# Splitting the first layer of a two-layer decoder step into two passes over the tokens, so that output projection and MLP of the first half may run beside the recurrent heads of the second

## The chip, the cores and the metric

One Trainium2 chip, all 8 cores, every core running the same program on its own prompt (2048 tokens) and 16 of the 128 sample tokens. The time is device microseconds (us) of the slowest core. A program on all cores has a second, slower state in some executions, in which the cores of a die get a lower clock. Ratios and their intervals below are of fast executions alone, against the kernel before in the same rounds. A median quoted for a run is over all its executions as the record has it; without the slow ones it changes by 1.3 us at most (late2, 1588.77 instead of 1590.04). The experiments ran in several rounds and on several chips, and the kernel before had fast medians of 1613.4 to 1614.8 us there, so a difference of a microsecond or two between two runs is not to be read. PE is TensorE, PEld its weight load, DVE VectorE, ACT ScalarE, POOL GpSimd, SP SyncE.

## The reference, cut to what matters

```python
def even_layer(h, ...):                          # layer 0; ... marks cuts
    proj = h @ w_in                              # 1024 -> 256 pool + 4 x 768
    pool_out, pool_new = pool_mix(u, ...)        # windows 2/4/8/16
    logf = jnp.log(lb32 + (1.0 - lb32) * jax.nn.sigmoid(fz32))
    k = (1.0 - lb32) * jax.nn.sigmoid(-fz32)
    v = jax.nn.silu(iz)
    o, s_new = hgrn2_chunked(q, k, v, logf, s_prev)   # 6 heads, 128 x 128 state, causal
    o = o * lax.rsqrt(jnp.mean(o * o, axis=-1, keepdims=True) + EPS)
    ...
    return jnp.concatenate([pool_out, o], axis=-1) @ w_out, pool_new, s_new

def trunk(x, ...):
    for l in range(2):
        h = rmsnorm(x, norm_mix[l])
        x = x + (even_layer if l == 0 else odd_layer)(h, ...)   # odd: a gated convolution of width 3
        h = rmsnorm(x, norm_mlp[l])
        x = x + jnp.square(jax.nn.relu(h @ ff_w1[l])) @ ff_w2[l]
    return rmsnorm(x, norm_final), ...
```

A tile is 512 tokens, so a prompt has tiles 0 to 3. A head's state runs through the tiles in order. Everything after the heads (projection, norm, MLP) is independent from token to token: that is what the change uses.

## The kernel before

The kernel is a generator of instructions. Each job (a head's work on one tile, a pool unit, the MLP) is a coroutine that yields operations. A list scheduler with a cost model picks, at each step, the operation that can start earliest by its estimates, and by priority where several are within 0.03 us. The result is one fixed order for each engine; on the chip each engine works its order off and waits, by semaphore, wherever an operand isn't there yet. So an estimate decides what stands behind what.

A unit is one head on one tile. It works in a context (five 2 KB pages a partition) and, at first, a gate buffer (three pages). Part of these pages lie in the arena, part in the place of x blocks ("x_sb"), which are reloaded later:

```python
def units():                                     # before
    for group in HEAD_GROUPS:                    # (0, 1), (2, 3), (4, 5)
        for t in range(4):
            for h in group:
                yield loaded(U_HEAD + h)
                yield h0(t)                      # tile t is normalised and transposed
                c = yield from take_c()          # one of 4 contexts
                itg = yield Alloc(gpool)
                # ... spawn core, gthread, vthread, gate at priorities 10 n .. 10 n + 3
                n += 1
```

The end of a unit, with the state, its write-out and the output:

```python
            yield STT(Sst[:, h, :], js(c.N, 2), c.r[:, 3:4], js(bank(kS), 3), ALU.mult, ALU.add, ...)
            flags.add(("S", h, t))
            # ... output matmuls
            if t == 3:
                yield ACT(js(c.N, 0), Sst[:, h, :], AF.Copy, [B_S[h]] + c.Br, c.BN, scale=c.r[:, 4:5])
                yield DMA("sp", misc(), [(nhp[h], js(c.N, 0))], c.BN, (), 65536)   # reads page N of the context
            yield ACT(c.kd, bank(ko), AF.Square, [B_ps[ko]], c.Bkd)
            # ...
            yield ACT(c.N, bank(km), AF.Ln, [B_ps[km]], c.BN, bias=EPS)            # writes page N again
            # ...
            yield STT(mixT[:, 2 + h, tokslice(t)], bank(ko), hcols[:, GAIN + h:GAIN + h + 1], c.lg, ALU.mult, ALU.mult, ...)
```

And the sequence of the dense parts, at the lowest priority (300):

```python
        def main():
            yield up(("G", HEAD_GROUPS[-1][-1], 2))
            banks.reserve([2, 3])
            yield from outproj(U_WO, 1, "mix")   # all 17 blocks: tiles 0 to 3 and the samples
            # ...
            mlp(U_FF0, 1, 2)                     # 8 steps x 5 tiles
            # ... conv, second projection, second MLP
```

Of the kernel before, what the change touches and what calls it, by code (L numbers as in the profile page):

```python
# [8 lines left out]
BF16 = mybir.dt.bfloat16  # L9
# [7 lines left out]
EPS = 1e-6  # L17
NSLOT = 5
NPG = 14
NXPG = 24  # L20
JUNK = [12, 13]
# [10 lines left out]
HEAD_GROUPS = [(0, 1), (2, 3), (4, 5)]  # L32
BLOCKS = list(range(17))
LAST_ORDER = (4, 0, 1, 2, 3)
LOAD_ORDER = [0, 1, 2, 3, 4, 5, 6] + list(range(7, 51))
LOAD_GATE = {1: 3, 2: 11, 3: 15, 4: 15}
XGATE = {b: (0,) for b in range(4, 16)}
POOLPRIO = -5
SMPPRIO = -5

U_HEAD = 0
U_POOL = 6
U_WO = 7
U_FF0 = 9
U_CONV = 25
U_OO = 33
U_FF1 = 35
NU = 51
# [308 lines left out]
def build():  # L357
# [40 lines left out]
    with ExitStack() as es:  # L398
# [174 lines left out]
        slot_pool = Pool([(i, [B_ring[i]]) for i in range(NSLOT)])  # L573

        def loader():
            for u in LOAD_ORDER:
                it = yield Alloc(slot_pool)
                s = it[0]
                ncol = unit_cols[u]
                pairs = [(ring[:, s, c0:min(c0 + 2048, ncol)], wst[u, :, c0:min(c0 + 2048, ncol)])  # L580
                         for c0 in range(0, ncol, 2048)]
                gate = LOAD_GATE.get(u)
                if gate is not None:
                    yield up(("x", gate))
                yield DMA("pool", ring_ds[s], pairs, [B_x[gate]] if gate is not None else [], [B_ring[s]], ncol * 512)
                slot_of[u] = s

        def loaded(*us):
            return Until(lambda: all(u in slot_of for u in us))

        def drop(u):
            s = slot_of.pop(u)
            slot_pool.give((s, [B_ring[s]]))

        def used(u, n):
            uses[u] = uses.get(u, 0) + 1
            if uses[u] == n:
                drop(u)
# [8 lines left out]
        def setup():  # L607
            yield from xload(0)
            yield DMA("sp", misc(), [(identb[:, :], c_identb), (gcols[:, :], gcols_d)], (), [B_const], 50000)
            flags.add("const")  # L610
            yield from xload(1)
            yield DMA("sp", misc(), [(lbl[:, :], lbl_d), (hcols[:, 18:24], gain_d)], (), [B_lbl, B_hcols], 12000)
            flags.add("small")
            yield from xload(2)
            yield from xload(3)
# [26 lines left out]
        def setup3():  # L642
            yield DMA("pool", ones_ds, [(onesb[:, :], c_onesm)], (), [B_ones], 65536)
            flags.add("ones")
            yield Until(lambda: U_HEAD + 2 in slot_of)
# [7 lines left out]
        junks = Pool([((i, JUNK[i]), [B_pg[JUNK[i]][0], B_pg[JUNK[i]][1]]) for i in range(len(JUNK))])  # L653
# [79 lines left out]
        def make_g(p0):  # L733
            g = Ctx()
            g.a, g.b, g.c = (pgf(p0 + k) for k in range(3))
            g.Ba, g.Bb, g.Bc = (list(B_pg[p0 + k]) for k in range(3))
            g.bufs = flat(pgb(p0, 3))
            return g
# [44 lines left out]
        def gthread(h, t, sl, c, g, key):  # L783
# [31 lines left out]
            gpool.give((g, g.bufs))  # L815
# [88 lines left out]
        NCU = 24 + 8 + 2  # L904

        def cgive(c):

            cpool.give((c, c.bufs))
            if cwait[0] == 0:
                for q in list(cpool.avail):  # L910
                    cpool.avail.remove(q)
                    for p in range(q[0].p0, q[0].p0 + 5):
                        flags.add(("pgdone", p))
                    cdone[0] += 1

        cwait = [NCU]
        cdone = [0]

        def take_c():
            it = yield Alloc(cpool)  # L920
            cwait[0] -= 1
            if cwait[0] == 0:
                for q in list(cpool.avail):
                    cpool.avail.remove(q)
                    for p in range(q[0].p0, q[0].p0 + 5):
                        flags.add(("pgdone", p))
                    cdone[0] += 1
            return it[0]

        def units():  # L930
            n = 0
            for group in HEAD_GROUPS:
                for t in range(4):
                    for h in group:
                        yield loaded(U_HEAD + h)
                        yield h0(t)
                        if n == 0:
                            yield up("hcols", "ones")
                        c = yield from take_c()
                        itg = yield Alloc(gpool)  # L940
                        sl = slot_of[U_HEAD + h]
                        key = (h, t)

                        def wrap(gen, h=h):
                            yield from gen
                            used(U_HEAD + h, 13)
                        S.spawn(core(h, t, c, key), 10 * n)
                        S.spawn(wrap(gthread(h, t, sl, c, itg[0], key)), 10 * n + 1)
                        S.spawn(wrap(vthread(h, t, sl, c, key)), 10 * n + 2)
                        S.spawn(wrap(gate(h, t, sl, c, key)), 10 * n + 3)  # L950
                        n += 1

        def gdone():
            yield Until(lambda: len(gpool.avail) == len(Gs) and ("G", HEAD_GROUPS[-1][-1], 3) in flags)
            for p0 in GPAGES:
                for p in range(p0, p0 + 3):
                    flags.add(("pgdone", p))
# [4 lines left out]
        def sample_hgrn():  # L962
            for gi, group in enumerate(HEAD_GROUPS):
                for h in group:
                    yield from sample_head(h)
# [3 lines left out]
        def sample_head(h):  # L969
            yield loaded(U_HEAD + h)  # L970
# [3 lines left out]
            sl = slot_of[U_HEAD + h]  # L974
# [4 lines left out]
            for g in range(4):  # L979
                yield DMA("sp", misc(), [(Sh[:, 4 * g:4 * g + 4, :], st_hgrn[4 * g:4 * g + 4, h].rearrange("b k v -> k b v"))],  # L980
                          (), pgb(shp + g), 262144)
# [12 lines left out]
            used(U_HEAD + h, 13)  # L994
# [27 lines left out]
            for g in range(4):  # L1022
# [9 lines left out]
                Bg = pgb(shp + g)  # L1032
                Sg = Sh[:, 4 * g:4 * g + 4, :]
# [8 lines left out]
                yield ACT(sbg, Sh[:, 4 * g:4 * g + 4, :], AF.Copy, Bg, Bsb)  # L1042
                yield MMG([(bank(ko)[:, 4 * g + i:4 * g + i + 1], sbg[:, i, :], qT[:, 4 * g + i:4 * g + i + 1], True, True)
# [14 lines left out]

        def pool_mixer(cch):
            yield loaded(U_POOL)  # L1060
            yield up("wblk")
            yield up(*[("h0", b) for b in range(17)])
            sl = slot_of[U_POOL]
            for t in range(4):
                yield from pool_unit(cch, t, sl)
            yield from pool_sample(cch, sl)

        def pool_unit(c, t, sl):
            cx = yield from take_c()
# [68 lines left out]
            cgive(cx)  # L1138
# [10 lines left out]
        def pool_sample(c, sl):  # L1149
            cx = yield from take_c()  # L1150
# [10 lines left out]
            used(U_POOL, 2)  # L1161
# [31 lines left out]
            cgive(cx)  # L1193


        def outproj(u0, norm_n, tag):
            yield loaded(u0, u0 + 1)
            s0, s1 = slot_of[u0], slot_of[u0 + 1]
            for b in BLOCKS:
                t = b // 4  # L1200
                yield up(*[(tag, c, t) for c in range(8)])
                if norm_n == 1 and b < 16 and b >= 16 - NXPG // 2:
                    yield up(("xback", b))
                it = yield Alloc(PB)
                p = it[0]
                pp = psT[p]
                tk = slice(b * 128, (b + 1) * 128) if b < 16 else slice(NT, NTOK)
                np_ = 128 if b < 16 else 16
                mms = []
                for half, s in ((0, s0), (1, s1)):  # L1210
                    for kc in range(8):
                        mms.append((pp[0:np_, half * 512:(half + 1) * 512], mixT[:, kc, tk],
                                    ring[:, s, kc * 512:(kc + 1) * 512], kc == 0, kc == 7))
                yield MMG(mms, mixb(t) + [B_ring[s0], B_ring[s1]], it[1])
                flags.add((tag + "used", b))

                def fin(b=b, p=p, it=it, np_=np_, pp=pp):
                    xb = x_sb[:, b, :] if b < 16 else xs_sb[0:16, :]
# [3 lines left out]
                S.spawn(fin(), 250)  # L1222
            drop(u0)
            drop(u0 + 1)


        hid = [[pgf(HIDP + 2 * i + n // 2).bitcast(BF16)[:, (n % 2) * 512:(n % 2 + 1) * 512] for n in range(4)]
               for i in range(NHID)]
        B_hid = [[B_pg[HIDP + 2 * i + n // 2][n % 2] for n in range(4)] for i in range(NHID)]
# [3 lines left out]
        def mlp(u0, n_in, n_out):  # L1233
            mtag = "m%d" % n_in
            steps = [(s, t) for s in range(8) for t in ((0, 1, 2, 3, 4) if s < 7 else LAST_ORDER)]
            hin = "h%d" % n_in
            pk_of = {}
            pi = 0
            for (s, t) in steps:
                if t < 4:  # L1240
                    pk_of[(s, t)] = pi
                    pi += 1

            def ff1():
                for s, t in steps:
                    yield loaded(u0 + 2 * s)
                    sl = slot_of[u0 + 2 * s]
                    yield up(*([(hin, b) for b in range(4 * t, 4 * t + 4)] if t < 4 else [(hin, 16)]))
                    if t < 4:
                        q = pk_of[(s, t)]  # L1250
                        if q >= NHID:
                            yield up((mtag, "hfree", q - NHID))
                        hb, Bh = hid[q % NHID], B_hid[q % NHID]
# [34 lines left out]
                    used(u0 + 2 * s, 5)  # L1288

            def ff2():  # L1290
                for s, t in steps:
                    yield loaded(u0 + 2 * s + 1)
                    sl = slot_of[u0 + 2 * s + 1]
                    if t < 4:
                        q = pk_of[(s, t)]
                        yield up(*[(mtag, "hid", q, n) for n in range(4)])
                        hb, Bh = hid[q % NHID], B_hid[q % NHID]
# [303 lines left out]
```

## Time and profile before

| | before |
|---|---|
| median of 4 runs | 1613.45 us (1612.48 to 1614.44) |
| profiled spans of the 8 cores | 1601.0 to 1610.6 us |
| granted clock, mean of a core | 0.980 to 0.984 |
| end of the first MLP, over the cores | 872.8 to 878.4 us, median 876.0 |

The prediction shows the main lines of the profile and reads them; three more are needed here. They are from the page of the kernel before: the queue of the weight loads (packets, MB, share of 16 DMA engines), the bytes read, and the loads of the weight ring (count, size, median us to landing).

```profile
q0 software_dynamic: 15008, 50.93, 18.9%
...
HBM read 124.20 MB, written 15.54 MB: 87 GB/s over the span
...
ring<-wst POOLq DMA_DIRECT2D x93, 512.0 KB, 8.4
```

The weight stream has room on average: its packets took less than a fifth of the time of the 16 DMA engines.

Two countings recur below. *PE work* is the number of matmuls times 217 ns for 512 columns, 61 ns for 128 and 30 ns for the small ones, close to the prediction's yardstick (an estimate: 32 of 512 columns take 6.94 us, 32 of 128 are listed with 1.95). *Lost* is a stretch's length less that work. It counts idle PE and low clock alike. The yardstick is a little generous: the 1.95 us include the modelled end of the last matmul, and from start to start the medians in these traces are 216, 56 and 25 ns. By the medians, more is lost in each stretch; the second set of numbers below says how much. The trace of before lacks 159 of 8932 matmul records, so its work up to the end of the first MLP is taken from the changed kernel's complete trace: 786.6 us, the same matmuls (the counts by size agree, but for 88 missing ones of 512 columns).

### The profile page before, as it was taken

The numbers are of one execution on the slowest core, as the hardware profiler recorded it, in microseconds if no ns is written. First come the engines' busy times: TensorE is split into PE (matmuls) and PEld (weight loads), VectorE is DVE, ScalarE is ACT, GpSimd is POOL, SyncE is SP. The second block draws the span as 40 slices with busy tenths as digits, with TensorE's granted clock in tenths as the row PEclk, the third lists the DMA queues.
The fourth block names the chain that finished last, engine by engine and source line by source line (L and its number), as shares of the span: only waits on it lengthen the run. The fifth ranks groups of instructions, "written<-read, shape, count | busy, mean of one in ns | idle before, by whom it ended". The sixth has DMA issues, their size and how long they took to land.

```text
span 1610.6 us, 23082 instructions; the slowest of 8 cores (1601.0 to 1610.6 us)
## 1 busy us (share of the span) xinstructions
PE 1512.9 (94%) x8773; PEld 742.5 (46%) x8932; DVE 935.7 (58%) x1396; ACT 603.6 (37%) x1222; POOL 179.7 (11%) x210
## 2 busy tenths in 40 slices
PE   3897698999999999999999999999999999999997
PEld 2554354555444444444445434445444444444443
DVE  4898686976454444444457555556544454444457
ACT  4786476876311111111148222236311111111135
POOL 1246733410000000000000000000000000000000
PEclk9898799999999999999999999999999999999999
DMA  9624235044321121122022023330320221121013
GB/s 238 138 61 89 62 78 112 29 89 127 52 53 27 27 53 31 22 52 47 1 40 40 4 40 50 55 66 1 53 53 8 45 53 27 27 53 27 1 54 157
DMA packets 51751, 90.32 MB, mean 56 GB/s; under 512 B 5422, under 2 KB 32924, under 8 KB 51644
## 3 DMA queue, kind: packets, MB, share of 16 engines
q0 software_dynamic: 15008, 50.93, 18.9%
q1 hardware_dynamic: 36636, 37.91, 7.7%
q8 instruction: 74, 1.21, 0.3%
q14 instruction: 33, 0.27, 0.1%
HBM read 124.20 MB, written 15.54 MB: 87 GB/s over the span
## 4 chain that ended last, share of the span: by engine, by line
PE 85%; DVE 6%; DMA 4%; ACT 2%; issue 2%; POOL 1%; SPq 0%; ACTq 0%; DVEq 0%; POOLq 0%
PE pp L516 83%; PE pp L526 2%; DVE arena L497 1%; DVE x_sb L485 1%; DVE arena L485 1%; DMA x_sb<-xp 1%; DMA ring<-wst 1%; ACT arena L472 1%; DMA nhp<-x_sb 1%; ACT x_sb L472 1%; DMA ncp<-arena 1%; DVE x_sb L497 0%; DMA ncs<-arena 0%; POOL x_sb L485 0%; SPq L531 0%
## 5 line engine op out<-in xcount | busy, mean ns | idle before, releaser
L516 PE MATMUL pp<-hT,ring 128*128 128x512 bf16 (+1 forms) x4018 | 792.0, 349 | 9.9 <-ACT arena L472 2.0
L516 PEld LDWEIGHTS pp<-hT,ring 128*128 128x128 bf16 x4112 | 353.2, 98 | 408.6 <-issue 29.8
L472 ACT ACTIVATE arena<-pp 128x512 bf16<-128x512 f32 (+4 forms) x370 | 211.5, 575 | 760.6 <-PE pp L516 732.8
L485 DVE TENSOR_TENSOR x_sb<-x_sb,pp 128x1024 f32<-128x1024 f32 (+1 forms) x312 | 367.8, 1179 | 189.4 <-PE pp L516 181.0
L516 PE MATMUL pp<-ring,arena 128*128 128x512 bf16 x2003 | 449.1, 379 | 3.8 <-DVE arena L485 1.4
L485 DVE TENSOR_TENSOR arena<-arena 128x512 bf16<-128x512 bf16 (+5 forms) x303 | 128.0, 424 | 322.9 <-ACT arena L472 309.8
L516 PEld LDWEIGHTS pp<-ring,arena 128*128 128x128 bf16 x2048 | 199.7, 98 | 242.5 <-issue 2.2
L531 POOL DMA_DIRECT2D ring<-wst x101 | 54.2, 542 | 1136.1 <-PE pp L516 1047.6
L516 PE MATMUL pp<-ring,mixT 128*128 128x512 bf16 (+1 forms) x529 | 121.2, 379 | 2.0 <-DVE x_sb L485 1.2
L473 ACT ACTIVATE arena<-x_sb 128x1024 bf16<-128x1024 f32 x64 | 67.6, 1056 | 58.2 <-DVE x_sb L485 57.2
L485 DVE TENSOR_TENSOR hT<-pp,gcols_s 128x1024 bf16<-128x1024 bf16 (+1 forms) x68 | 78.5, 1164 | 15.5 <-PE pp L526 15.4
L516 PEld LDWEIGHTS pp<-ring,mixT 128*128 128x128 bf16 (+1 forms) x544 | 51.6, 97 | 58.9 <-issue 1.5
L472 ACT ACTIVATE x_sb<-x_sb 128x512 f32<-128x512 f32 (+3 forms) x126 | 69.9, 570 | 8.8 <-DVE x_sb L485 7.6
L516 PE MATMUL pp<-ring,hT 128*128 128x128 bf16 (+2 forms) x896 | 64.4, 229 | 0.5 <-ACT mixT L472 0.4
L485 DVE TENSOR_TENSOR arena<-pp,arena 128x512 f32<-128x512 f32 (+3 forms) x63 | 36.5, 582 | 48.0 <-PE pp L516 31.1
L497 DVE SCALAR_TENSOR_TENSOR arena<-arena,convwf_s 128x512 f32<-128x512 f32 x64 | 48.0, 750 | 21.4 <-ACT arena L472 20.2
L485 POOL TENSOR_TENSOR x_sb<-x_sb 128x512 f32<-128x512 f32 x40 | 50.0, 1249 | 68.3 <-DVE x_sb L485 25.8
L516 PEld LDWEIGHTS pp<-ring,hT 128*128 128x128 bf16 (+1 forms) x896 | 53.2, 97 | 8.8 <-issue 3.6
L472 ACT ACTIVATE x_sb<-pp 128x512 f32<-128x512 f32 (+5 forms) x104 | 46.3, 457 | 27.8 <-PE pp L516 17.2
L472 ACT ACTIVATE arena<-x_sb,nrm 128x1024 bf16<-128x1024 f32 x48 | 54.8, 1145 | 1.2
L485 POOL TENSOR_TENSOR arena<-arena 128x512 f32<-128x512 f32 (+6 forms) x36 | 44.2, 1228 | 40.0 <-DVE gsm L502 13.6
L516 PE MATMUL pp<-x_sb 128*128 128x128 bf16 (+2 forms) x325 | 32.4, 220 | 14.9 <-DVE x_sb L485 5.6
(110 smaller groups left out, 760.4 us busy)
## 6 DMA issues: line engine op xcount, KB each, us to landing
ring<-wst POOLq DMA_DIRECT2D x93, 512.0 KB, 8.4
x_sb<-xp SPq DMA_DIRECT2D x28, 512.0 KB, 13.2
yp<-x_sb SPq DMA_DIRECT2D x16, 512.0 KB, 2.6
x_sb<-st_hgrn SPq DMA_DIRECT2D x24, 256.0 KB, 7.3
nhs<-x_sb SPq DMA_DIRECT2D x24, 256.0 KB, 2.4
ring<-wst POOLq DMA_DIRECT2D x8, 256.0 KB, 6.9
arena<-gfin SPq DMA_DIRECT2D x1, 512.0 KB, 3.8
ncs<-arena SPq DMA_DIRECT2D x16, 8.0 KB, 1.5
```

The lines of the kernel that those rows point to most:

```text
L472: return e.activation(out=out, in_=in_, func=func, bias=bias, scale=scale)
L473: return e.activation(out=out, in_=in_, func=func, bias=bias, scale=scale, accum_out=accum)
L485: return Op(eng, lambda e: e.tensor_tensor(out=out, in0=in0, in1=in1, op=op), R, W, occ, occ + 0.08)
L497: return Op("dve", lambda e: e.scalar_tensor_tensor(out=out, in0=in0, scalar=scalar, in1=in1, op0=op0, op1=op1), R, W, occ, occ + 0.08)
L516: ins = e.matmul(o, l, r, start=s, stop=t)
L526: ins = e.transpose(out=o, in_=i, identity=idn)
L531: fns = [(lambda e, o=o, i=i: e.dma_start(out=o, in_=i)) for (o, i) in pairs]
```

## The change

Its intent: in the kernel before, PE has nothing but units while units run. The change orders the units so that tiles 0 and 1 are finished for all six heads first. Then projection and MLP of these two tiles (the *filler*) can run beside the units of tiles 2 and 3. The price is that the weights of four heads, of the projection and of the MLP come from HBM twice. Cut to the core (each `...` is a cut):

```diff
-HEAD_GROUPS = [(0, 1), (2, 3), (4, 5)]
+FIRST_HEADS = (0, 1, 2, 3, 4, 5)
+LATER_HEADS = (4, 5, 0, 1, 2, 3)
+UNITS = [(h, t, 0) for h in FIRST_HEADS for t in (0, 1)] + \
+    [(h, t, 0 if h in FIRST_HEADS[4:] else 1) for h in LATER_HEADS for t in (2, 3)]
+RETIRE = {12: NPG + 8, 22: NPG + NXPG}          # contexts given back to x at these units
...
-LOAD_GATE = {1: 3, 2: 11, 3: 15, 4: 15}
-XGATE = {b: (0,) for b in range(4, 16)}
+LOAD_GATE = {(0, 1): 7, (0, 2): 7, (0, U_POOL): 11, (0, 3): 15}
+XGATE = {b: ((0, 0),) if b < 8 else ((0, 2),) for b in range(4, 16)}
 POOLPRIO = -5
-SMPPRIO = -5
+SMPPRIO = 145
+NORMPRIO = 25
+POOLT = 2                                       # pool units of tiles 0, 1 early, in a page of their own
...
         def main():
-            yield up(("G", HEAD_GROUPS[-1][-1], 2))
+            yield from outproj(0, U_WO, 1, "mix", range(8), True)
+            mlp(0, U_FF0, 1, 2, (0, 1), (0, 1), hid_a, True)
+            yield up((("m1", 0), "done"), ("S", LASTHEAD, 2))
             banks.reserve([2, 3])
-            yield from outproj(U_WO, 1, "mix")
+            yield from outproj(1, U_WO, 1, "mix", range(8, 17), False)
...
-            mlp(U_FF0, 1, 2)
+            mlp(1, U_FF0, 1, 2, (2, 3, 4), (4, 2, 3), hid_b, False)
```

The weight loader becomes two streams (units first, dense parts behind), which share the five ring slots. The first pass evicts half blocks from single PSUM banks, as the pairs are still in use by the units.

## The prediction

> **What bounds the kernel now.** I read the summary of the profile first (busy time, then 40 slices), then the stretches by stage, then PE's waits and the ends of the recurrent heads.
>
> ```profile
> PE 1512.9 (94%) x8773; PEld 742.5 (46%) x8932; DVE 935.7 (58%) x1396; ACT 603.6 (37%) x1222; POOL 179.7 (11%) x210
> PE   3897698999999999999999999999999999999997
> DVE  4898686976454444444457555556544454444457
> PEclk9898799999999999999999999999999999999999
> ```
>
> PE is nearly full from the ninth slice (one slice is 40.3 us) to the last. Its holes lie in the first eight, where the recurrent layer runs and DVE is as full as PE. The stretches say this in us (columns: length, then busy time of PE, weight load, DVE, ACT, POOL, then clock, DMA share, GB/s):
>
> ```profile
> 0.00:40.00 40.00, 14.19 (x112) 10.04 (x114) 17.80 (x29) 19.44 (x50) 4.26 (x10) 0.97 0.96 237
> 40.00:138.00 98.00, 86.97 (x784) 53.87 (x794) 85.91 (x168) 77.35 (x176) 35.72 (x37) 0.90 0.55 110
> 138.00:200.00 62.00, 43.79 (x334) 23.82 (x338) 46.99 (x89) 31.97 (x69) 45.28 (x38) 0.83 0.20 53
> 200.00:346.00 146.00, 131.82 (x1161) 79.32 (x1174) 117.32 (x245) 114.09 (x245) 53.16 (x48) 0.96 0.33 68
> 346.00:886.00 540.00, 534.73 (x2870) 252.60 (x2925) 283.08 (x340) 166.80 (x312) 19.05 (x36) 1.00 0.24 48
> 886.00:1010.00 124.00, 116.13 (x536) 51.99 (x545) 69.39 (x141) 29.44 (x56) 4.21 (x8) 0.99 0.19 31
> ```
>
> 346 to 886 us is the first output projection and MLP: PE 99%, granted clock 1.00. Before 346 us PE is busy for 276.8 us and idle for 69. The idle time has no single owner; these are its causes between 28 and 340 us, and the worst moment:
>
> ```profile
> PE pp L516 <- ACT x_sb L472: 15.3, 12, 6.6
> PE pp L516 <- DVE arena L485: 7.4, 3, 4.9
> PE pp L516 <- DVE x_sb L485: 5.6, 5, 2.0
> ...
> 272.11 1.09 ACT L472 ACTIVATE x_sb<-pp 128x512 f32<-128x512 f32 x2 [8.35 <-DMA nhp<-x_sb]
> ```
>
> The last line is a dependency between two head units, not work: a state on its way out held the page that the next unit needed. The writes of the state Sst, one for each of 24 units (6 heads x 4 token tiles), give the pace: units 2 to 9 end between 78.31 and 150.31 us, 9 us each; then one ends only at 197.15 us, because the pool mixers (first in priority) took the unit contexts and ran their POOL chains; the last ends at 356.49.
>
> **Pages of the Trainium skill.**
> 1. "Perfetto Trace Analysis", section "Per-instruction lifecycle": the end of a matmul is estimated, so busy time is a poor measure. The trace agrees: a 128x512 matmul lists 379 ns, but 32 of them in the MLP take 6.94 us, 217 ns each. I therefore count PE work by spacing.
> 2. "TensorE: Matmul & The Clock Gate", "Part 1: The HAM clock gate": idle time lowers the clock. The trace agrees for thin stretches (0.83 in 138 to 200). The same part expects a 13/16 clock once three cores of a die run dense matmuls; here it is 1.00 on dense stages, and all cores average 0.980 to 0.984, so the measurement decides: denser filling costs no clock.
> 3. "VectorE: DVE Perf Modes", section on the TRN2 errata: a fixed cost for each instruction. The trace agrees in direction: the PSUM add of 128x512 f32 takes 676 ns, that of 128x1024 takes 1220, so two halves cost 132 ns more.
> 4. "DMA: Bandwidth & Descriptors", the fit in "Anatomy of one DMA": 2.0 us + bytes/436e3, 3.2 us for 512 KB. The weight loads here land after 8.4 us (median), so I use that.
>
> **The change, part by part.**
> (a) Units now go head by head over tiles 0 and 1 for all six heads, then tiles 2 and 3. After the first 12 units, output projection and MLP of tiles 0 and 1 may fill PE while the other 12 units run. Later the same weights are loaded again for tiles 2, 3 and the samples.
> (b) Four pool units and both pool samples work in a scratch page, and the sample heads drop in priority and prefetch their states.
> (c) Start: constants first, then blocks 0 to 3; blocks 8 to 15 wait for the third head's weights, so blocks 4 to 7 come sooner.
> (d) Contexts shrink from 4 to 3 after unit 12 (pages go back to x).
> (e) The first pass evicts half blocks into single banks.
>
> PE work, by spacing. A unit: 24 matmuls of 512 columns x 217 ns = 5.2 us; 32 of 128 columns in 1.95 us; about 20 small ones at 57 ns and one of 217 = 1.35; in all 8.5 us, x24 = 204. Pool: 72 x 217 ns = 15.6. Norm transposes: 8. Sample heads: about 4 us each (estimate from their counts), 24. Sum 252 us. The dense stage 346 to 886 adds 540 including 3 to 5 us of idle. The recurrent stage lasts 346 us, so it loses 346 - 252 = **94 us of PE**. The change removes none of the PE work: it can only recover part of these 94.
>
> First half, before any filler exists. DVE's instructions sum to 9.0 us a unit; neighbours overlap, and sum against union over this stage is 311 to 281, so 8.15 us. 12 units 98, 17 norms 30, four pool units and two pool samples 16, setup 2: 146 us of DVE. About 18 are done by 30 us if blocks 4 to 7 come early; the other 128 at the 91% that DVE reaches between 60 and 120 us take 141: the 12th unit ends at 171, and the projection of tile 0 may start near 165. PE has then done 11.3 units (96) + norms 8 + pool 8 = 112 us: **53 us are lost** in 165 and stay lost, against 63 by a like count in the kernel before at 175 us. Here filler has no work to do, so this caps the gain at 94 - 53 = 41.
>
> Second half. PE: 12 units 102, pool 8, samples 24, projection of 8 blocks 128 x 217 ns = 28, MLP 8 x 2 x 64 x 217 ns = 222, norms 8: 392 us. DVE: 98 + 9 + 26 + adds 144 x 0.61 = 88 + squares 24 + hT evictions 18 = 263 (67%). ACT about 190. So PE bounds the half as a whole. But the units come first in priority: while they are in flight (some 165 us), units, samples and pool need 133 us of DVE and 134 of PE, and the gap is all that filler gets, with another 12 of DVE. DVE then stands near 88% and PE should stand near 95. The instruction order of each in-order queue is fixed beforehand; each late chain stops PE although MLP matmuls stand behind. I estimate 9% lost over 165 us, 15, and 3 more for one stall of the nhp kind: **18 us lost**. The remaining MLP of the first pass is as dense as now.
>
> Extra transfers: 4 head units, 2 of Wo, 16 of the MLP, 22 in all, two issues each: 93 issues of 512 KB become about 137, HBM reads 124 become some 170 MB. An MLP step on two tiles lasts 27.7 us and needs four loads; at 8.4 us landing and the 18.9% share that 50.9 MB cost, they are hidden. Half evictions add 144/2 x 0.132 = 9.5 us of DVE, hidden too.
>
> Sum: 94 - 53 - 18 = 23 us gained; 2 us given back at seams (a second projection, fewer norm buffers). 1613.45 - 21 = **1592 us**, 1.3% faster.
>
> **The rivals.**
> A. Filler closes nearly everything (second half loses 8, first half 50): gain 36, 1577 us. For it: PE waits in the dense stages are below 1%. Against: those have chains of two instructions, these units of twenty; the conv stage, whose chains are longer, keeps PE at 116.13 of 124 us.
> B. The order backfires: 3 contexts instead of 4, and relu and adds of the MLP queue ahead of unit work on DVE and ACT, so units stretch and both lose 35 us: 1609 us.
> C. Transfers bite: the 10.6 us of waiting for the nhp write came while weights were loading (DMA share 0.84 in 260 to 270 us). With twice the weight stream in the second half, six such writes and reloads of x, three stalls of 8 us cost 24: 1613 us, no gain. Against it: only one of six did so now.
>
> **Range and chances.** The middle is 1592. 1577 (A) is near the best case, 1610 (B, or half of C) near the worst that I expect: 1576 to 1610. Faster by over 2% means under 1581.2, which needs 32 of the 41 us possible: 0.18. Slower by over 2%, over 1645.7, needs all gains lost and 32 more: 0.02. Within 2%: 0.80.
>
> **What would show it.** Right: the same dense stages after about 600 us; PE idle plus low clock still in the first 165 us; projection matmuls (ring, mixT) first near 165 us, between unit matmuls; PE 90 to 95% until the 24th write of Sst near 340; about 137 large ring loads. The end of the first MLP, 886 before, should come near 865. Wrong: if PE is under 88% in 165 to 340 (B), if ACT waits long on nhp or PE on ring loads (C), or if the first 12 units end well before 160 or after 185, which moves the cap itself.

## The result, and the profile after

| | before | after |
|---|---|---|
| median | 1613.98 us (13 runs, 2 of them slow) | 1575.17 us (8 runs) |
| profiled spans of the cores | 1601.0 to 1610.6 | 1568.1 to 1573.3 |
| granted clock | 0.980 to 0.984 | 0.992 to 0.995 |
| end of the first MLP, median core | 876.0 | 844.6 |

Ratio 0.9764, 95% interval 0.9754 to 0.9774: faster by 2.4%, 38 us, where 21 had been predicted, and 1 us outside the range. A ratio is the mean time of one kernel's fast runs over that of the other's fast runs of the same rounds, so it isn't quite the ratio of the medians quoted.

The page of the changed kernel, same parts as before (busy time, 40 slices, queue, bytes, ring loads):

```profile
PE 1508.4 (96%) x8932; PEld 737.0 (47%) x8932; DVE 936.9 (60%) x1468; ACT 597.8 (38%) x1222; POOL 204.1 (13%) x254
...
PE   3889999999999999999999999999999999999997
...
DVE  4898888887544565454446566556445444444467
...
PEclk9999999999999999999999999999999999999999
...
q0 software_dynamic: 21344, 74.00, 28.3%
...
HBM read 170.34 MB, written 15.54 MB: 118 GB/s over the span
...
ring<-wst POOLq DMA_DIRECT2D x137, 512.0 KB, 8.3
```

PE's busy time is the same to 0.3%; the work was moved, not saved. The holes that stood in the first eight slices now stand in the first three. 44 more ring loads and 46 MB more came as predicted, and a load still lands in 8.3 us: the transfers show no cost here.

The stretches of the changed kernel (length, then busy time of PE, weight load, DVE, ACT, POOL, then clock, DMA share, GB/s). The cuts are: first projection matmul, last state write, end of the first MLP, first matmul of the second projection, end of the second MLP:

```profile
0.00:180.90 180.90, 139.53 (x1215) 86.27 (x1216) 139.01 (x276) 126.08 (x274) 49.19 (x53) 0.96 0.55 116
180.90:355.40 174.50, 170.72 (x1416) 97.47 (x1415) 145.89 (x290) 132.42 (x292) 83.78 (x80) 1.00 0.56 117
355.40:845.70 490.30, 485.95 (x2652) 225.96 (x2652) 262.12 (x369) 137.38 (x267) 47.92 (x78) 1.00 0.44 82
845.70:1030.50 184.80, 181.14 (x879) 82.41 (x877) 107.39 (x211) 52.31 (x99) 8.45 (x16) 1.00 0.24 39
```

The same for before, from the end of its first MLP to the second projection:

```profile
877.20:1067.80 190.60, 182.08 (x861) 82.80 (x879) 108.12 (x210) 52.26 (x100) 8.43 (x16) 0.99 0.23 37
```

The second line of the changed kernel is the result: 12 units, the sample heads and the filler together keep PE busy for 170.7 of 174.5 us at full clock. By PE work, 130.6 of the first 180.9 us is work (50.3 lost), 169.8 of the next 174.5 (4.7 lost), and all but 4.1 of the 490.3 after that. The three losses add to 59.1 up to the end of the MLP; before it was 877.2 - 786.6 = 90.6. So 31.5 us were gained by there. (With the median spacings the three are 54.9, 9.5 and 8.8, and before is 105.2: the gain stays at 32, but the second half then lost 9.5 us, not 4.7.) The rest is 733.4 us before and 727.6 after on the two profiled cores (731.2 and 727.1 on the median core), so 4 to 6 us more came after it.

What PE still waited for in the second stretch (total, times, longest, in us):

```profile
PE pp L531 <- DMA ring<-wst: 1.0, 1, 1.0
PE pp L541 <- ACT arena L487: 0.9, 1, 0.9
PE pp L531 <- POOL x_sb L500: 0.9, 2, 0.5
PE pp L531 <- ACT x_sb L487: 0.4, 1, 0.4
PE pp L531 <- DVE Sst L512: 0.3, 1, 0.3
```

One wait of 1.0 us for a weight load (the prediction's rival C), and 0.3 us for a state update. Twelve chains of twenty dependent instructions run in this stretch, and all waits together are 3.5 us.

### The profile page after: what moved, and what is told of

The parts are those of the page before. It is cut to its first block, busy times and chain, and to the rows that moved or that the text cites. A ratio compares the mean times of both kernels' runs of the same rounds, so it can differ in the third digit from the quotient of the medians.

```text
span 1573.3 us, 23472 instructions; the slowest of 8 cores (1568.1 to 1573.3 us)
## 1 busy us (share of the span) xinstructions
PE 1508.4 (96%) x8932; PEld 737.0 (47%) x8932; DVE 936.9 (60%) x1468; ACT 597.8 (38%) x1222; POOL 204.1 (13%) x254
## 4 chain that ended last, share of the span: by engine, by line
PE 86%; DVE 6%; DMA 3%; ACT 2%; issue 1%; POOL 1%; SPq 0%; DVEq 0%; ACTq 0%; POOLq 0%
PE pp L531 84%; PE pp L541 2%; DVE x_sb L500 1%; DVE arena L500 1%; ACT arena L487 1%; DMA x_sb<-xp 1%; DVE x_sb L512 1%; ACT x_sb L487 1%; DVE arena L512 1%; DMA ring<-wst 1%; DMA ncp<-arena 1%; DVE hT L500 1%; POOL x_sb L500 0%; DMA arena<-convw 0%; DVE x_sb L819 0%
## 5 line engine op out<-in xcount | busy, mean ns | idle before, releaser
L487 ACT ACTIVATE arena<-pp 128x512 bf16<-128x512 f32 (+3 forms) x319 | 182.3, 576 | 596.4 <-PE pp L531 565.1
L531 PE MATMUL pp<-ring,arena 128*128 128x512 bf16 x1536 | 339.3, 379 | 3.6 <-DVE arena L500 3.6
L500 DVE TENSOR_TENSOR arena<-arena 128x512 bf16<-128x512 bf16 (+3 forms) x236 | 98.9, 421 | 243.7 <-ACT arena L487 234.3
L531 PE MATMUL pp<-ring,mixT 128*128 128x512 bf16 (+1 forms) x1056 | 238.6, 379 | 1.9 <-DVE x_sb L500 1.0
L531 PEld LDWEIGHTS pp<-ring,arena 128*128 128x128 bf16 x1536 | 149.7, 98 | 184.8 <-issue 4.2
L531 PEld LDWEIGHTS pp<-ring,mixT 128*128 128x128 bf16 (+1 forms) x1056 | 100.3, 97 | 118.2 <-issue 5.2
L487 ACT ACTIVATE mixT<-pp 128x512 bf16<-128x512 f32 (+1 forms) x72 | 39.3, 549 | 141.0 <-PE pp L531 131.5
L500 POOL TENSOR_TENSOR x_sb<-x_sb 128x512 f32<-128x512 f32 (+6 forms) x56 | 70.3, 1255 | 76.8 <-DVE gsm L500 31.1
L500 DVE TENSOR_TENSOR mixT<-mixT 128x512 bf16<-128x512 bf16 x64 | 30.0, 468 | 71.9 <-ACT mixT L487 71.7
L487 ACT ACTIVATE arena<-arena 128x512 f32<-128x512 f32 x88 | 53.7, 623 | 5.1 <-DVE arena L512 4.4
```

Of the source, the lines that this page charges most:

```text
L487: return e.activation(out=out, in_=in_, func=func, bias=bias, scale=scale)
L500: return Op(eng, lambda e: e.tensor_tensor(out=out, in0=in0, in1=in1, op=op), R, W, occ, occ + 0.08)
L531: ins = e.matmul(o, l, r, start=s, stop=t)
```

## The experiments

The theory: the filler is what closes the holes, and it takes nothing from the units, because the order of instructions places it where a unit's chain leaves PE free. Rivals: (1) much of the gain is from other parts of the change (the start, the priorities, the scratch page for pooling); (2) the change gains because one stall of before, the held page, happens not to occur. All runs below gave correct results.

**1. Reordered units without filler (nofill).** The first projection waits for the last unit.

```diff
         def main():
+            yield up(*[("mix", 2 + h, 3) for h in range(6)])
             yield from outproj(0, U_WO, 1, "mix", range(8), True)
```

> The changed kernel, but the first projection and MLP of tiles 0 and 1 wait until all 24 head units are done; new start, pool scratch and two passes stay. Theory F (the gain of the second half is the MLP matmuls that stand between the head units): the 24 units end earlier than 354 us, 330 to 345, but the dense work begins only then, and the time is 1595 to 1612 us. Theory P (the gain is mostly the pool mixers and sample heads that no longer take contexts, and the new start): under 1588 us.

Measured: 1639.95 us, ratio 1.0163 (1.0147 to 1.0179). Its stretches:

```profile
0.00:180.00 180.00, 139.92 (x1209) 85.98 (x1210) 138.89 (x275) 125.56 (x273) 49.07 (x53) 0.96 0.52 118
180.00:360.00 180.00, 139.00 (x1113) 78.76 (x1110) 118.71 (x248) 110.15 (x245) 80.87 (x76) 0.85 0.42 101
360.00:420.00 60.00, 58.67 (x354) 28.55 (x355) 35.66 (x57) 32.49 (x69) 13.59 (x16) 0.92 0.52 119
```

From 180 to 360 us PE has 112.9 us of work (67 lost, at clock 0.85), against 4.7 lost with filler. Its 24th state write falls at 348 to 361 us over the cores, where 330 to 345 was expected; in the changed kernel it falls at 350 to 355. So the units end no earlier when the filler is away: in sum the filler costs them nothing. (It also raises the granted clock, 0.85 to 1.00; the runs don't separate the two.) The filler is worth 1639.95 - 1575.17 = 65 us. The reordering without it costs 26 against before, where theory F had expected no loss (1595 to 1612). In part this is because before overlaps its own last units with its projection: from 331 us to its last unit's end it runs 77 matmuls of the projection, 17 us. The rest of the 26 is not taken apart. The net is the 38 us seen. Every rival in which the other parts carry the gain falls here.

**2. The start and the pool units.** Three runs: the changed kernel with the old gates and norm priority (startold; the order of the constants stays new), before with the new start (start_before), and the changed kernel with no pool units ahead (poolt0).

```diff
-NORMPRIO = 25
+NORMPRIO = 1
-LOAD_GATE = {(0, 1): 7, (0, 2): 7, (0, U_POOL): 11, (0, 3): 15}
-XGATE = {b: ((0, 0),) if b < 8 else ((0, 2),) for b in range(4, 16)}
+LOAD_GATE = {(0, 1): 3, (0, 2): 11, (0, 3): 15, (0, 4): 15}
+XGATE = {b: ((0, 0),) for b in range(4, 16)}
```

> The changed kernel with the old gates of the first transfers and the old (high) priority of the norms. Theory F: the new start gives the 12th state write some 5 to 10 us, so without it 1580 to 1586 us. If the start were worth nothing: 1573 to 1577. If it carried the gain (theory P): 1590 or more.

Measured: 1589.34 us, ratio 0.9848 (0.9831 to 0.9865), 14 us slower than the changed kernel and between the two expectations. The 12th unit ends at 184 to 187 us over the cores instead of 175 to 179, and the 24th at 371 to 376 instead of 350 to 355.

```diff
 # kernel before: constants ahead of x, blocks 8 to 15 behind the second head's weights, norms at priority 25
-XGATE = {b: (0,) for b in range(4, 16)}
+XGATE = {b: (0,) if b < 8 else (1,) for b in range(4, 16)}
...
-            S.spawn(norm0x(k, 4), 1 + k)
+            S.spawn(norm0x(k, 4), 25 + k)
```

> The kernel before with the new start (constants first, blocks 8 to 15 after the second head's weights, norms below the first units). Undoing the start cost the changed kernel 14 us. If the start is worth as much by itself: 1597 to 1604 us. If the gain needs the filler behind it (a shifted unit alone only moves waiting): 1608 to 1618.

Measured: 1609.74 us, ratio 0.9985 (0.9958 to 1.0011): at most 7 us, and no difference shown. (Three of the four executions took 1608.6 to 1609.9 us, one 1621.64.)

```diff
-POOLT = 2
+POOLT = 0
```

> The changed kernel with the pool units of tiles 0 and 1 in unit contexts again instead of the scratch page. Theory P: the mixers hog contexts in the first half, the 12th state write moves from 178 to 200 us or more and the time to 1590 us or more. Theory F: the first half gets 5 to 12 us longer and little is made good later: 1578 to 1588 us.

Measured: 1597.93 us, ratio 0.9903 (0.9888 to 0.9919), 23 us slower than the changed kernel. The 12th unit ends at 190 to 195 us, not the 200 of theory P, but the time is in its range (1590 or more): these pool units in the unit contexts do cost that much while filler waits behind them. The first MLP ends at 858 to 868 us.

What follows: the new start is worth 14 us in the changed kernel and no shown amount in before. When filler waits behind the 12th unit, 8 us at the start are paid later as well. These parts help the filler; without it, the reordered kernel that has them all is slower than before (nofill).

**3. Priorities in before (prio_before).** The largest hole of before follows from its pool mixers going first. Put them, and the samples, last:

```diff
-POOLPRIO = -5
-SMPPRIO = -5
+POOLPRIO = 145
+SMPPRIO = 145
```

> The kernel before with pool mixers and sample heads at low priority, all else as before. If the hole from 150 to 197 us was the mixers holding the contexts and this alone is worth a lot (theory P): under 1600 us. Theory F: the hole only moves, since these units need contexts and DVE at some time: 1600 to 1618 us.

Measured: 1630.25 us, ratio 1.0105 (1.0087 to 1.0122). That is slower than before and than both expectations. The 24th state write comes at 300 us instead of 356, but nothing is won:

```profile
180.00:300.00 120.00, 99.97 (x861) 58.76 (x872) 91.80 (x204) 84.30 (x187) 49.84 (x47) 0.90 0.40 84
300.00:332.00 32.00, 26.73 (x135) 11.84 (x139) 19.12 (x31) 14.98 (x30) 18.52 (x16) 0.79 0.24 60
332.00:357.00 25.00, 15.04 (x119) 7.83 (x117) 19.75 (x27) 13.09 (x31) 19.57 (x18) 0.88 0.47 84
```

The units finish 56 us earlier and leave pool and sample chains alone at the end, with PE at 15 of 25 us. A hole that comes from chains moves when the chains are reordered. It closes only with work that doesn't depend on them.

**4. How much of the result is the order itself.** Scale the scheduler's cost model for ACT, DVE and POOL by 0.7, in both kernels, and by 1.15 in the changed one. The instructions stay the same; their order changes.

```diff
         self.eng, self.fn, self.R, self.W = eng, fn, flat(R), flat(W)
+        if eng in ("act", "dve", "pool") and dma is None:
+            occ, lat = 0.7 * occ, 0.7 * lat
         self.occ, self.lat, self.multi, self.dma, self.margin = occ, lat, multi, dma, margin
```

> The changed kernel, with the instruction order computed as if VectorE, ScalarE and GpSimd were 30% faster than the ordering assumes, so that each head chain is placed too early on PE. Theory O (fixed order, late chains stop PE): the second half loses 20 us or more, 1593 us or more. Theory F with slack: PE, the slowest engine there, lags behind the plan and chains are in time: 1580 us or less.

> The kernel before with the order computed as if VectorE, ScalarE and GpSimd were 30% faster. The same edit cost the changed kernel 96 us. If a wrong order hurts because MLP matmuls stand behind each late chain, the kernel before, with no MLP there, loses less: 1630 to 1665 us. If it hurts all in-order queues alike, 1690 or more.

> The changed kernel with the order computed as if VectorE, ScalarE and GpSimd were 15% slower, so PE gets more MLP matmuls ahead of each head chain. If the order of the changed kernel is already in time (1 to 2% of PE lost in the second half), nothing is left to win and the units only end later: 1572 to 1582 us. If late chains still cost 10 us or more somewhere before 355 us: 1560 to 1568.

Measured: the changed kernel at 0.7, 1671.32 us, ratio to before 1.0356 (1.0338 to 1.0375); before at 0.7, 1669.57, 1.0347 (1.0329 to 1.0365); the changed kernel at 1.15, 1604.29, 0.9934 (0.9922 to 0.9946). So a wrong estimate costs the changed kernel 96 us, before 56, and with the bad estimates nothing of the change's gain is left. The run at 1.15 missed both expectations: placing the filler earlier costs 29 us too, of which its trace shows one wait of PE of 7.6 us for a weight load; the rest is not explained. The changed kernel at 0.7, cut at its first projection matmul and its last unit:

```profile
0.00:209.00 209.00, 144.45 (x1177) 85.75 (x1177) 151.61 (x280) 125.26 (x270) 60.00 (x64) 0.93 0.48 103
209.00:385.00 176.00, 156.18 (x1321) 88.48 (x1322) 131.02 (x266) 128.03 (x282) 69.53 (x67) 0.97 0.49 102
385.00:420.00 35.00, 22.70 (x150) 10.73 (x148) 15.97 (x31) 11.71 (x27) 8.49 (x11) 0.85 0.78 145
```

In the second line PE is busy for 156 of 176 us, 89%, with the very filler that gives 98% in the delivered order. PE loses 31 us there instead of 4.7, much of it in waits of up to 1.9 us on ACT and DVE: a late chain does stop PE although filler stands behind it, as the prediction said. (That is some 26 of the 96 us; some 30 more are lost before 209 us.) The delivered order has hardly a late chain.

**5. Other orders of the changed kernel.** Only tile 0 in the first pass (split1); the last two heads of the first half tile by tile (late2); two contexts and one gate buffer in the second half (ctx2).

```diff
 # split1, cut
-UNITS = [(h, t, 0) for h in FIRST_HEADS for t in (0, 1)] + \
-    [(h, t, 0 if h in FIRST_HEADS[4:] else 1) for h in LATER_HEADS for t in (2, 3)]
+UNITS = [(h, 0, 0) for h in FIRST_HEADS] + \
+    [(h, t, 0 if h in FIRST_HEADS[4:] else 1) for h in LATER_HEADS for t in (1, 2, 3)]
...
-            mlp(0, U_FF0, 1, 2, (0, 1), (0, 1), hid_a, True)
+            mlp(0, U_FF0, 1, 2, (0,), (0,), hid_a, True)
```

> A new version: only tile 0 of all six heads first, then its projection and MLP as filler, tiles 1 to 3 after it. The loss of the first half ends at the 6th state write instead of the 12th, so it should fall from 49 to about 38 us: 1562 to 1570 us. If the weight stream (a pair of loads for each 14 us of filler) or too little filler (125 us) binds instead: 1576 or more.

Measured: 1639.56 us, ratio 1.0164 (1.0144 to 1.0184), a miss. The two largest holes of core 1 as stretches, and then what ended the waits of ACT, of POOL (a sample head) and of PE in them (start, duration, instruction, in brackets the idle time before it and what ended it):

```profile
240.00:260.00 20.00, 1.05 (x7) 0.30 (x6) 4.57 (x10) 5.35 (x11) 5.78 (x7) 0.50 0.87 160
420.00:440.00 20.00, 11.02 (x52) 4.49 (x50) 6.25 (x13) 3.42 (x8) 5.51 (x7) 0.83 0.94 188
...
256.95 0.60 ACT L487 ACTIVATE arena<-pp 128x512 f32<-128x512 f32 x1 [12.19 <-DMA nhp<-arena]
...
426.79 1.04 POOL L500 TENSOR_TENSOR x_sb<-x_sb 128x512 f32<-128x512 f32 x1 [9.89 <-DMA x_sb<-st_hgrn]
...
429.55 0.24 PE L531 MATMUL pp<-x_sb 128*128 128x1 bf16 x4 [7.99 <-ACT x_sb L487]
```

With one tile for each pair of loads the DMA share stands at 0.87 and 0.94 there, and the transfers do bite (rival C). On this core PE waits for no weight load, though: it waits behind a state write that holds a page (experiment 6) and behind a sample head's state load, both of which came late among the weights. Core 6 has the long wait on a state write too; the other six cores have one wait of PE of 6.7 to 9.5 us for a weight load. The two holes cost some 30 us of the 64 between this run and the changed kernel; the rest is spread over other stretches.

```diff
 # late2
-UNITS = [(h, t, 0) for h in FIRST_HEADS for t in (0, 1)] + \
+UNITS = [(h, t, 0) for h in FIRST_HEADS[:4] for t in (0, 1)] + [(h, t, 0) for t in (0, 1) for h in FIRST_HEADS[4:]] + \
```

> The changed kernel, but the last two heads of the first half run tile 0 of both, then tile 1 of both, so that tile 0 is complete after 10 units, not 11, and its projection can start some 9 us earlier. If the lost time of the first half is only lack of ready matmuls: 1568 to 1573 us. If the order is set by something else (weights of the projection in the ring): 1574 to 1580.

Measured: 1590.04 us, ratio 0.9841 (0.9828 to 0.9854), some 14 us slower than the changed kernel and outside both expectations. The projection starts sooner, at 168 to 175 us instead of 177 to 182, but the cores end anywhere between 1571 and 1590, with ACT waits of 1.2 to 6 us on small state writes on six of them, waits for weights, and POOL waits on state loads.

```diff
 # ctx2
-RETIRE = {12: NPG + 8, 22: NPG + NXPG}
+RETIRE = {12: NPG + NXPG}
```

> The changed kernel with only 2 unit contexts (3 before) and one gate buffer in the second half. Theory F (ready MLP matmuls stand in front of every late chain, so PE does not care how late a unit is): the 24th state write moves from 354 to beyond 380 us, PE stays over 96% busy, time 1572 to 1581 us. Theory O, of the prediction (fixed order, each late chain stops PE): fewer units in flight mean more stops, 1587 us or more.

Measured: 1590.32 us, ratio 0.9856 (0.9841 to 0.9872). By its time that is theory O. But the cores fall in two groups, both of them on both dies: cores 1, 2, 4 and 6 span 1570.6 to 1572.5 us, cores 0, 3, 5 and 7 span 1585.7 to 1588.4.

The fast four end as the changed kernel does, although their 24th unit ends at 404 to 406 us, 50 later: on these cores slow units cost nothing, as theory F says. The slow four each have one long wait on ACT, 12.1 to 12.5 us; the fast four wait 0.2 to 0.6 us at the same place. Core 0, in the same columns:

```profile
227.68 0.25 ACT L487 ACTIVATE arena<-pp 15x128 f32<-15x128 f32 x1
...
247.31 0.60 ACT L487 ACTIVATE arena<-pp 128x512 f32<-128x512 f32 x1 [12.46 <-DMA npp<-arena]
```

The first line writes 15 rows of pool state into a corner of a context's page; a write-out of 7.5 KB reads them there; the next unit that gets the page waits until it is done. All of ACT stands still for 12.5 us, and with it the MLP's evictions, so filler can't hide it. From 180 to 300 us PE is busy for 103 us here, against 115 on core 1.

**6. The held page by itself.** The same kind of wait stands in before, 5.5 to 8.3 us on every core, and the prediction shows it, but takes it for one between two units. The code above says otherwise: after the write-out reads page N, the unit's own norm (`AF.Ln`) writes page N again, and it is this instruction that waits. In the chain of work that ended last, before reads (start, us, what):

```profile
260.96 0.48 ACT x_sb L472 x2
...
261.50 10.59 DMA nhp<-x_sb
```

Is the held page a cost of its own, or only where late chains show? All runs so far changed the order of instructions too. So the small writes were given memory of their own, with the order on every engine unchanged (the traces agree, instruction by instruction). The head state is scaled in place in Sst and sent from there; the pool rows go through unused partitions of the samples' x tile:

```diff
-                yield ACT(js(c.N, 0), Sst[:, h, :], AF.Copy, [B_S[h]] + c.Br, c.BN, scale=c.r[:, 4:5])
-                yield DMA("sp", misc(), [(nhp[h], js(c.N, 0))], c.BN, (), 65536)
+                yield ACT(Sst[:, h, :], Sst[:, h, :], AF.Copy, [B_S[h]] + c.Br, c.BN + [B_S[h]], scale=c.r[:, 4:5])
+                yield DMA("sp", misc(), [(nhp[h], Sst[:, h, :])], [B_S[h]], (), 65536)
+                for q in c.BN:                   # the scheduler's estimate stays as it was
+                    q.rt = max(q.rt, B_S[h].rt)
...
-                yield ACT(stg, bank(k)[0:15, 0:128], AF.Copy, [B_ps[k]], [Bf])
-                yield DMA("sp", misc(), [(npp[:, c * 128:(c + 1) * 128], stg)], [Bf], (), 7680)
+                yield ACT(xs_sb[32:47, c * 128:(c + 1) * 128], bank(k)[0:15, 0:128], AF.Copy, [B_ps[k]], [Bf, B_npp[c]])
+                yield DMA("sp", misc(), [(npp[:, c * 128:(c + 1) * 128], xs_sb[32:47, c * 128:(c + 1) * 128])], [B_npp[c]], (), 7680)
+                Bf.rt = max(Bf.rt, B_npp[c].rt)
```

> The kernel before, with the small state write-backs (six nhp, two npp) sent from memory of their own (nhp from Sst scaled in place, npp from unused partitions of the samples' x tile) instead of from a unit's page; the order of instructions on every engine is unchanged. Theory (a held page is a stall of its own, on top of what the chains cost): the ACT wait of 5 to 8 us on the nhp write is gone on all cores and the kernel gains 5 to 8 us, 1605 to 1609. Rival (the chains that follow were late anyway, the wait only names the last of several): the wait's place is taken by another and the gain is under 2 us, about 1613.

Measured: 1608.07 us, ratio 0.9962 (0.9933 to 0.9991): 7 us by the medians, 1 to 11 by the interval. The first MLP ends at 868.4 to 870.7 us over the cores, 6 earlier. The instruction that waited 8.35 us in before now follows at once (core 6, same columns as above):

```profile
263.74 0.62 ACT L472 ACTIVATE x_sb<-x_sb 128x512 f32<-128x512 f32 x1
264.26 1.07 ACT L472 ACTIVATE x_sb<-pp 128x512 f32<-128x512 f32 x2
```

> The changed kernel with two unit contexts in its second half (ctx2, 1590), and its small state writes from memory of their own, same order. Theory (the slow cores of ctx2 are slow through the held page of one npp write alone): all eight cores end near 1571 to 1574, no ACT wait over 3 us on npp or nhp. Rival (two contexts are too few and the wait is only where it shows): the slow cores stay above 1583, idle on something else.

Measured: 1581.21 us, ratio 0.9799 (0.978 to 0.9818), 9 us faster than ctx2. The two groups are gone: all cores end between 1574.2 and 1579.8. So the page was the cause of the slow group. But 1571 to 1574 was expected: 6 us against the changed kernel remain, spread over all cores. Their cause stays open.

> The changed kernel with its last two heads of the first half interleaved by tile (late2, 1590), small state writes from memory of their own, same order. Theory: the part of its 15 us that came from waits on nhp and npp (1.4 to 6 us a core) goes: 1578 to 1584; its waits on weight loads and on st_hgrn stay. Rival (the order is simply worse): above 1587.

Measured: 1587.1 us, ratio 0.9829 (0.9807 to 0.9852), only 2 to 3 us faster than late2 where 1578 to 1584 was expected. The rival's bound (above 1587) is just met or just missed, depending on whether slow executions count in the median (1586.71 without them), so most of the loss is of the order itself. PE waits up to 3.6 us at a time for weights in it.

> The changed kernel with its small state writes from memory of their own, same order. Its waits on nhp and npp sum to under 3 us a core, so theory and rival both say 1571 to 1576; if it were over 5 us faster, the changed kernel too had hidden stalls of this kind.

Measured: 1575.19 us, ratio 0.9761 (0.9742 to 0.978), as the changed kernel. Its ACT waits on the head states sum to 3.0 us, and none of it was worth anything.

What follows: a held page is a cost of its own, 7 us in before and 9 in ctx2. The changed kernel, in its delivered order, has none of it left. Rival (2) is right about its share: of the 38 us, about 7 could have been had in before by eight small writes from other memory.

**7. The seam behind the first MLP (seamgate).** In the changed kernel the convolution may start as soon as its own tile is normalised, and tiles 0 and 1 have long been. Make it wait for all:

```diff
             n = 0
+            yield up(*[("h2", b) for b in range(17)])
             order = [(c0 + i, t) for c0 in range(0, 8, NCONV) for t in range(4) for i in range(NCONV)]
```

> The changed kernel, but the convolution waits for the norms of all blocks, not only those of its own tile. The stage from the end of the first MLP to the second projection took 184.8 us, 190.6 before. If that gain comes from tiles 0 and 1 being normed long ago: 4 to 8 us slower, 1579 to 1583. If it is only how the small sample chains fell in the order: 1573 to 1577.

Measured: 1581.14 us, ratio 0.9796 (0.9783 to 0.9809), 6 us slower than the changed kernel. From the end of the first MLP to the end takes 729.7 us on the median core, against 727.1 in the changed kernel and 731.2 before. So this start is worth some 6 us in all, as expected if it matters. Where the gain lies is less sure: 2.6 of the 4.1 us gained behind the MLP would come from it, but the same stretch takes 724.8 us in ctx2 and late2, so 2 us of difference come about in other ways too. The rest stays open, and so does what this edit costs ahead of the MLP's end (some 3 of its 6 us).

## Why the prediction was right or wrong

The mechanism was right: PE work unchanged, the first half not helped, filler in the second half, transfers hidden. The size was wrong, 21 us instead of 38. "Faster by over 2%" had been given a chance of 0.18. By the terms of the sum:

| term | predicted, us | measured, us |
|---|---|---|
| lost while the recurrent layer runs, before | 94 | 91 (the dense part from 346 us on lost nothing by this count) |
| lost in the first half, after | 53 up to 165 | 50.3 up to 180.9 |
| lost in the second half, after | 18 | 4.7 |
| gained up to the end of the first MLP | 23 | 31.5 |
| lost in the rest of the first MLP, after | not counted | 4.1 |
| seams | -2 | +4 to +6 |

**The step that failed** is the second half: "I estimate 9% lost over 165 us, 15, and 3 more for one stall of the nhp kind". It lost 4.7 of 174.5 us, 2.7%, counted with the prediction's own spacings (9.5 us, 5.4%, with the median ones): the waiting was overestimated, and the stall of the nhp kind did not come (ACT waits 3.0 us in all on head states). The 9% was a guess with no measurement behind it; the nearest stretch that the prediction names, the convolution stage, had 116.13 of 124 us busy. Both of its grounds are real: late chains stop PE in experiment 4, and a held page stops ACT in ctx2. They simply don't happen in the delivered order. Other orders of the same design (old start, late2, ctx2) land at 1589 to 1590 us, close to the 1592 predicted. One may read this as having priced a typical order where the delivered one is better; no run shows that this was the error.

The kernel before already had the evidence. From 331 us on its last units ran beside its projection. That is the situation of the second half, and the stretch reads:

```profile
332.00:357.00 25.00, 24.84 (x169) 13.47 (x171) 20.79 (x38) 17.77 (x38) 3.47 (x5) 1.00 0.60 109
```

PE 24.84 of 25 us at clock 1.00, with DVE at 83%. I had cut the stages at 346 us and took this for the start of the dense part. Rival A should have had more than the role of a best case: it has 50 and 8 lost where the runs show 50.3 and 4.7, and its 1577 us is 2 us from the result.

**First half.** The end of the 12th unit was put at 171 us and the start of the projection near 165; they came at 178.2 and 180.9. The loss is right nonetheless, since more work (130.6 us instead of 112) was done by then: two errors that cancel, which is luck. Experiment 2 shows how sharp this cap is: with the old start the 12th unit ended 8 us later and the kernel 14.

**Seams.** "2 us given back" had the wrong sign. The prediction counted a second projection and fewer buffers, and missed that two tiles are normalised long before the MLP ends, which lets the convolution start at once (experiment 7; how much of the 4 to 6 us that is stays open).

**Transfers.** 137 loads and 170 MB, as predicted, landing in 8.3 us. Hidden, with two tiles for each load; with one tile they aren't (split1), and even with two a single small write can come late (ctx2).

**Units.** Rival B's first ground, that filler ahead of them would stretch the units, is refuted by nofill: they end at the same time with and without filler. Its second, three contexts instead of four, was not tried by itself; with two, four cores lost nothing (ctx2).

**Smaller slips.** Units 2 to 9 of the kernel before end 10.3 us apart, not 9 (72 us in seven steps); rival C adds up to 1616 us, not 1613. Neither entered the sum.

## What to carry to other kernels

When long dependent chains leave an engine idle, look for work on other data that doesn't depend on them; reordering the chains only moves the hole. Before pricing such an overlap by guess or analogy, look in the trace for a stretch in which the two kinds of work already run side by side, and read the loss there. A small write-out from a working page that is written again can stop an engine for many times the write's usual length (12.5 us in ctx2, where the other such write landed in 1.4): send it from memory that nothing else waits for.

## What the Trainium skill lacked or had wrong

- "TensorE: Matmul & The Clock Gate", section "Back-to-back issue gap": it gives 131 ns a matmul as the sustained spacing at 512 columns and 81 ns at 128. In these traces the median from start to start is 216 and 56 ns (changed kernel, 180.9 to 355.4 us, clock 1.00), which is what the page's isolated formula gives.
- The same page, "Part 1: The HAM clock gate": the 13/16 clock that it expects once three cores of a die run dense matmuls isn't seen in the fast executions profiled here: 1.00 on the dense stretches of both kernels, and 0.992 to 0.995 as the mean of the changed one. In slow executions the mean clock of a die falls as low as 0.845 (late2_stage, 1829.37 us); no profile of one was kept, so whether that is this limit stays open.
- "DMA: Bandwidth & Descriptors" has no figure for how late a small write is done when bulk loads surround it. A 7.5 KB write, issued at 228.0 us in ctx2 with the DMA share at 1.00 until 247.3, released its waiter only at 247.31, 19 us later; the other such write, issued at 209.0, landed in 1.4. Eight loads of 512 KB were issued within 6 us of it, and a 256 KB state write issued 1.7 us before it landed at 246.6. The 512 KB loads of the changed kernel land in 8.3 us (median); the page's fit in "Anatomy of one DMA", which is per DMA, gives 3.2.
- I found no page that prices what such a write holds up. Memory of its own for eight small writes gained 7 us in the kernel before (ratio 0.9962) and 9 us in ctx2, with the order of instructions unchanged.
